# Attention's residual made in the gate stage, and down projections that open with two fetched pages and fetch the rest among their weights

## The chip, the cores and the metric

The kernel is one program on one of the eight cores of a Trainium2 chip. The metric is the time of one execution on the device in microseconds (us); three executions of the kernel before are at hand, and one more was taken by the hardware profiler.

The engines have short names here: PE (TensorE, matrix products), DVE (VectorE), ACT (ScalarE), POOL (GpSimd) and SP (SyncE, which in this kernel issues every DMA, in the order of its program).

## What is computed

Two layers over 1024 tokens of width 1024, in float32. Layer 0 mixes tokens with a gated MLP, layer 1 with a neighbourhood attention; each layer goes on with a convolutional FFN and a gate:

```python
for i in range(DEPTH):
    mix = spatial_gating_mixer(x, ...) if i % 2 == 0 else neighbourhood_attention(x, ...)   # o @ w_o + b_o
    x = layer_norm(DEEPNORM_ALPHA * x + mix, ln1_g[i], ln1_b[i])
    ffn = conv_ffn(x, ...)          # (gelu(a) * g) @ w_down + b_down, hidden width 2816 = 22 pages of 128
    x = layer_norm(DEEPNORM_ALPHA * x + ffn, ln2_g[i], ln2_b[i])
    gate = jax.nn.sigmoid(x @ ple_w_gate[i] + ple_b_gate[i])
    x = x + gate * (p[i] @ ple_w_proj[i])
```

So attention's residual is ALPHA times the output of layer 0's gate, plus the bias b_o.

## The kernel before, in words

**Products.** Each float32 operand is split in two parts, `hi` (a rounded copy, made by ACT, line 90) and `lo` (the remainder, made by DVE, line 91). `mm3` (lines 113 to 118) makes a product from three matmuls: hi by hi, hi by lo, lo by hi. A matmul here has 512 columns. A "page" is 128 of the contracted channels for all 1024 tokens, 512 KB.

**Order.** The program is written with a tile library that puts instructions in order on each engine and inserts the waits; a tile with a tag has a fixed number of buffers (`wr`, raw weights, 2; `wh` and `wl`, split weights, 3 each; `bc` 3), and a new tile waits until the oldest buffer's readers are done. Eight semaphores serve the DMAs in turn, so SP issues one only when the DMA eight before it has landed.

**finish, tm_part1, tm_part2** (lines 425, 169 and 203) are the last step of each mixer and of each FFN: a product with tokens on the partitions, residual, layer norm. `tm_part1` runs over two column halves h, and in each over the pages `ks` but the last three, two pages to a chunk: a chunk's weights are loaded to `wr` and split, the two pages are split into a ring of eight buffers in a big tile, and PE runs 48 matmuls (8 token blocks, 2 pages, 3 each). The four PSUM tiles of a half are then added to `acc` by DVE, eight additions (line 201), and only this frees them for the other half. `acc` is filled beforehand with the residual: a DMA for each of 8 token blocks, and a DVE operation ALPHA * acc + bias (line 421). The first page of the mixers without a reordered store, and of the FFN, is split into two `bc` buffers named `yf` (line 428). `tm_part2` does the last three pages and the layer norm.

**ffn** (line 516) makes the up projection in 22 steps; from step 3 on each is seven products of half size (`seven`, line 454), followed by the convolution, gelu and gate in `evac` (line 574). Pages 0 to 19 of the result go to DRAM (`yd`), 20 and 21 stay in SBUF. The down projection takes its pages in the order 20, 21, 18, 19, 0 to 17; lines 615 to 623 first issue the DMAs that fetch all pages back, then the eight for `acc` (from `xb`, the layer norm's output), then call `finish`.

**ple** (line 628) is the gate. In layer 0 each of its eight channel blocks x is split for the next stage, transposed by PE (`turn`, line 674) and stored to DRAM as `xres`, tokens by channels.

**attention** (line 715) does eight head pairs. Their outputs are gathered by POOL in a tile `tmp` (line 866) and stored as page `oT[hp]`. After the last pair, lines 914 to 922 load `acc` from `xres` in eight DMAs, each a grid block of 8 rows by 16 tokens, make the residual with bias row R_BO, and load the eight `oT` pages to `yo`. `finish` then takes pages 0 to 4 in `tm_part1` and 5 to 7 in `tm_part2`.

Of the kernel before, what the change touches and what calls it, by code (L numbers as in the profile page):

```python
# [9 lines left out]
F32 = mybir.dt.float32  # L10
F32R = mybir.dt.float32r
AF = mybir.ActivationFunctionType
# [4 lines left out]
P = 128  # L17
T = 1024
D = 1024
NT = T // P  # L20
# [5 lines left out]
R = 3  # L26
ALPHA = 4.0 ** 0.25
# [7 lines left out]
C_GATE = C_QKV + 24  # L35
NCOL = C_GATE + 16


(R_BV, R_SG, R_SB, R_BS, R_BOUT, R_BO) = (0, 2, 4, 6, 7, 8)
R_L = 9  # L40


class Trunk:
# [123 lines left out]


    def tm_part1(self, w, y, ks, acc, ring, residual, prep):

        nc = self.nc
        i = ri = 0
        for h in range(2):
            pss = [self.ps() for _ in range(4)]
            for c in range(0, len(ks), 2):
                kk = ks[c : c + 2]
                wh, wl = self.chunk(w[h, kk[0] : kk[-1] + 1].rearrange("k p f -> p k f"), (P, len(kk), 512))
                yy = []
# [235 lines left out]

    def residual(self, acc, row):
        b = []

        def scale(t):
            if not b:
                b.append(self.row(row))  # L420
            self.nc.vector.scalar_tensor_tensor(acc[:, t, :], acc[:, t, :], ALPHA, b[0], op0=ALU.mult, op1=ALU.add)

        return scale

    def finish(self, ringslot, w, y, K, acc, residual, which, X, cols=None, xb=None):

        rg = self.slot(ringslot, F32R)
        first = xb is None and [self.wp.tile([P, T], F32R, tag="bc", name=self.name("yf"), bufs=3) for _ in range(2)]
        ring = lambda i: (rg[:, 2 * (i % 4), :], rg[:, 2 * (i % 4) + 1, :]) if i or not first else first
        ks = list(range(K)) if isinstance(K, int) else K  # L430
# [10 lines left out]

        self.tm_part1(w, y, ks[:-R], acc, ring, residual, prep)
        layer, ln2 = divmod(which, 2)
# [72 lines left out]
    def ffn(self, layer, X, old, new):  # L516
# [8 lines left out]
        B |= {n: (q(TH, i, j), q(TL, i, j)) for n, i, j in (("T1", 0, 0), ("T2", 0, 1), ("T3", 1, 0), ("T4", 1, 1))}  # L525
        HOME = {16: 2, 17: 4, 18: 3, 19: 5}
        cnt = {"wh": 0, "wl": 0}
# [87 lines left out]
        yb = [self.slot(new[0], F32), self.slot(new[1], F32)]  # L615
        ks = [20, 21, 18, 19] + list(range(18))
        for k in (18, 19, *range(18)):
            y[k] = yb[k // 8][:, k % 8, :] if k < 16 else self.single(HOME[k], F32)
            nc.sync.dma_start(y[k], yd[k])
        acc = self.slot(old[0], F32)  # L620
        for t in range(NT):
            nc.sync.dma_start(acc[:, t, :], self.xb[t])
        residual = self.residual(acc, R_L + 5 * layer + 2)
        return self.finish(old[1], a["w_down"][layer], lambda k: y[k], ks, acc, residual, 2 * layer + 1,
                           lambda: (self.slot(new[0], F32R), self.slot(new[1], F32R)))


    def ple(self, layer, X, new):
# [30 lines left out]
        def evac(j, ps, pj, sl=slice(0, T)):  # L659
            s = self.tmp()[:, sl]  # L660
            x = self.single(4 if new else (j + sl.start // 512) % 4, F32)[:, sl]
            nc.gpsimd.tensor_tensor(x, XH[:, j, sl].bitcast(F32), XL[:, j, sl].bitcast(F32), op=ALU.add)
            psf = ps.rearrange("p h f -> p (h f)")[:, sl]
            c = C_GATE + 8 * layer + j
            nc.scalar.activation(s, psf, AF.Sigmoid, bias=self.cols[:, c : c + 1])
            nc.vector.tensor_tensor(s, s, pj[:, sl], op=ALU.mult)
            nc.vector.tensor_tensor(x, x, s, op=ALU.add)
            if not new:
                nc.sync.dma_start(self.out[j][:, sl], x)
                return  # L670
            self.split(NH[:, j, :], NL[:, j, :], x)
            self.pend.append(lambda: turn(j, x))

# [41 lines left out]
    def attention(self, X, free, old):  # L715
        nc, a = self.nc, self.a
        fa, fb = self.slot(free[0], F32), self.slot(free[1], F32R)
        qk = [self.single(i, F32R) for i in range(6)]
        oT = self.dp.tile([8, P, T], F32, name="oT")
        fa = fa.rearrange("p k f -> p (k f)")  # L720
# [129 lines left out]
        def values(hp, t):  # L850
# [8 lines left out]
            if t == 0:  # L859
                st["o"] = self.tmp()  # L860
            o = osum[0:64, t % 2]
            nc.scalar.copy(o, ptf[64:128, 0:512])
            nc.vector.tensor_tensor(o, ptf[0:64, 0:512], o, op=ALU.add)
            for e in range(2):
                c = e * 256
                nc.gpsimd.tensor_tensor(st["o"][64 * e : 64 * e + 64, t * P : t * P + P], o[:, c : c + P], o[:, c + P : c + 256], op=ALU.add)
            if t == 7:
                nc.sync.dma_start(oT[hp], st["o"])
# [114 lines left out]
def prep(i):  # L983
# [3 lines left out]
    o = {}  # L987
# [51 lines left out]
    colv += [np.asarray(i["ple_b_gate"])[l] for l in range(2)]  # L1039
    o["cols"] = c(np.concatenate([v.reshape(-1, P) for v in colv]).T)  # L1040
    rows = [np.asarray(i["sg_b_in"])[0, E:], np.asarray(i["sg_ln_g"])[0], np.asarray(i["sg_ln_b"])[0],
            np.asarray(i["sg_b_s"])[0], np.asarray(i["sg_b_out"])[0], np.asarray(i["na_b_o"])[0]]
    for l in range(2):
# [21 lines left out]
```

## Time and profile before

| what | value |
|---|---|
| median of 3 executions | 2722.09 us (2720.78 to 2722.97) |
| the profiled execution's own time | 2721.23 us |
| its span, first to last instruction | 2719.5 us |
| mean granted TensorE clock | 0.994 of full |
| PE busy | 2671.1 us (98%) |
| DVE busy | 1714.2 us (63%) |
| ACT busy | 1086.1 us (40%) |
| DMA | 238.36 MB, mean 88 GB/s |

Times in the trace are counted from the first instruction. The time of an execution holds 1.7 us more than the span. An engine's row names the tile that it writes, then those that it reads, and in brackets how long the engine stood idle before it and what ended that; PE's clock is given as a share of the full 2.4 GHz. In this program layer 0's FFN ends its up projection at 998 us, layer 0's gate runs from 1282 to 1392 us, attention's last product begins at 1831 us, and layer 1's FFN ends its up projection at 2370 us.

### The profile page before, as it was taken

The page shows a single profiled execution, that of the slowest core. Times are in us where ns is not written, and L with a number is a line of the kernel's source. Part 1 is how long each engine was busy: PE and PEld are TensorE (multiplying, and loading weights), DVE is VectorE, ACT ScalarE, POOL GpSimd, SP SyncE. Part 2 cuts the span into 40 slices and gives each one's busy share as a digit, 9 for nine tenths or more (in the row PEclk, how much of TensorE's full clock was granted, in tenths as well). Part 3 has the DMA queues.
Part 4 walks back from the last instruction along what each step waited for, and adds up shares of the span by engine and source line. Part 5 has one row for each costly group of instructions (what it writes and reads, how often), then busy time and mean ns, then how long its engine had stood idle before and what let it go on. Part 6 is the DMA issues. An engine that isn't in the chain of part 4 may idle for free.

```text
span 2719.5 us, 31562 instructions
## 1 busy us (share of the span) xinstructions
PE 2671.1 (98%) x12536; PEld 2196.1 (81%) x12536; DVE 1714.2 (63%) x2223; ACT 1086.1 (40%) x1475; POOL 350.6 (13%) x372
## 2 busy tenths in 40 slices
PE   9999999999999999999999999997999999999999
PEld 7888888888888878888887777776888888788887
DVE  3247554498787864347437767685887877743373
ACT  3234222344444442224335555572444444522231
POOL 0013320010000000002124333340200000000031
PEclk9999999999999999999999999998999999999999
DMA  5111131222222263121321111154312222451113
GB/s 177 55 55 41 42 132 51 81 86 70 88 76 93 70 223 139 52 61 36 102 87 55 40 47 55 36 175 146 94 68 88 83 80 93 149 203 54 43 55 124
DMA packets 86660, 238.36 MB, mean 88 GB/s; under 512 B 7536, under 2 KB 19696, under 8 KB 86512
## 3 DMA queue, kind: packets, MB, share of 16 engines
q1 hardware_dynamic: 86512, 236.34, 25.6%
q8 instruction: 98, 1.61, 0.3%
q14 instruction: 50, 0.41, 0.0%
HBM read 190.18 MB, written 46.14 MB: 87 GB/s over the span
## 4 chain that ended last, share of the span: by engine, by line
PE 92%; DVE 4%; ACT 1%; DMA 1%; issue 1%; POOL 0%; SPq 0%; DVEq 0%; ACTq 0%
PE ps L116 20%; PE ps L118 20%; PE ps L117 20%; PE bank L117 9%; PE bank L116 9%; PE bank L118 9%; PE ps L845 1%; PE ps L857 1%; PE ps L827 1%; PE ps L235 1%; DMA bc<-in_rows 1%; ACT bigA L831 1%; DVE bigA L835 1%; DVE bigB L91 0%; ACT wh L90 0%
## 5 line engine op out<-in xcount | busy, mean ns | idle before, releaser
L91 DVE TENSOR_TENSOR wl<-wr,wh 128x1024 fp32r<-128x1024 f32 (+2 forms) x227 | 247.2, 1090 | 274.5 <-ACT wh L90 274.0
L90 ACT CAST wh<-wr 128x1024 fp32r<-128x1024 f32 (+2 forms) x227 | 212.1, 935 | 336.9 <-PE ps L117 136.8
L224 POOL TENSOR_SCALAR st<-st 128x1 f32<-128x1 f32 x32 | 34.1, 1065 | 1598.6 <-ACT ps L223 1598.6
L116 PE MATMUL ps<-wh,bigD 128*128 128x512 f32 x592 | 230.3, 389 | 0.0
L118 PE MATMUL ps<-wh,bigD 128*128 128x512 f32 x592 | 230.3, 389 | 0.0
L117 PE MATMUL ps<-wl,bigD 128*128 128x512 f32 x592 | 230.3, 389 | 0.0
L117 PE MATMUL ps<-bigD,wh 128*128 128x512 f32 x544 | 214.6, 394 | 0.0
L116 PE MATMUL ps<-bigA,wh 128*128 128x512 f32 x512 | 200.7, 392 | 0.9 <-DVE tmp L387 0.9
L118 PE MATMUL ps<-bigA,wl 128*128 128x512 f32 x512 | 199.4, 389 | 0.0
L116 PE MATMUL ps<-bigC,wh 128*128 128x512 f32 x480 | 199.2, 415 | 0.0
L118 PE MATMUL ps<-bigC,wl 128*128 128x512 f32 x480 | 190.5, 397 | 0.0
L118 PE MATMUL ps<-wh,bigB 128*128 128x512 f32 x456 | 178.3, 391 | 0.0
L117 PE MATMUL bank<-bigD,wh 128*128 128x512 f32 x456 | 177.4, 389 | 0.0
L116 PE MATMUL ps<-wh,bigA 128*128 128x512 f32 x336 | 133.0, 396 | 19.7 <-DVE bigC L201 14.8
L117 PE MATMUL ps<-bigB,wh 128*128 128x512 f32 x384 | 149.5, 389 | 0.0
L117 PE MATMUL ps<-wl,bigA 128*128 128x512 f32 x336 | 132.7, 395 | 0.0
L116 PEld LDWEIGHTS ps<-wh,bigD 128*128 128x128 f32 x592 | 111.1, 188 | 23.3
L117 PEld LDWEIGHTS ps<-wl,bigD 128*128 128x128 f32 x592 | 111.1, 188 | 23.0
L118 PEld LDWEIGHTS ps<-wh,bigD 128*128 128x128 f32 x592 | 111.1, 188 | 23.0
L116 PE MATMUL bank<-bigA,s 128*128 128x512 f32 x304 | 118.3, 389 | 0.0
L118 PE MATMUL bank<-bigA,s 128*128 128x512 f32 x304 | 118.3, 389 | 0.0
L116 PE MATMUL bank<-bigA,wh 128*128 128x512 f32 x304 | 118.3, 389 | 0.0
(286 smaller groups left out, 6371.2 us busy)
## 6 DMA issues: line engine op xcount, KB each, us to landing
wr<-in_w_up SPq DMA_DIRECT2D x88, 512.0 KB
wr<-in_w_down SPq DMA_DIRECT2D x42, 512.0 KB
yd<-s SPq DMA_DIRECT2D x40, 512.0 KB
wr<-in_w_qkv SPq DMA_DIRECT2D x24, 512.0 KB
bc<-in_rows SPq DMA_DIRECT2D x18, 512.0 KB
wr<-in_w_u SPq DMA_DIRECT2D x16, 512.0 KB
bigA<-yd SPq DMA_DIRECT2D x16, 512.0 KB
wr<-in_w_gate SPq DMA_DIRECT2D x16, 512.0 KB
```

The costliest lines, as they stand in the source:

```text
L90: self.nc.scalar.copy(hi, x)
L91: self.nc.vector.tensor_tensor(lo, x, hi.bitcast(F32), op=ALU.subtract)
L116: mm(out, lh, rh, start=start, stop=False)
L117: mm(out, lh, rl, start=False, stop=False)
L118: mm(out, ll, rh, start=False, stop=stop)
L224: nc.gpsimd.tensor_scalar(st[:, 3:4], st[:, 2:3], 1.0 / D, EPS, op0=ALU.mult, op1=ALU.add)
L235: nc.tensor.transpose(pt[:, kb], a[:, kb], self.ident)
L827: nc.tensor.matmul(ps[:, e, 0:n], qs[es, t * P : t * P + P], kv(ks, es), start=i == 0, stop=i == 2)
L831: nc.scalar.activation(L[:, e, 0:n], L[:, e, 0:n], AF.Exp, bias=sm[:, e : e + 1], scale=-1.0, accum_out=sm[:, 2 + e : 3 + e])
L835: nc.vector.tensor_scalar(L[:, e, 0:n], L[:, e, 0:n], sm[:, 4 + e : 5 + e], None, op0=ALU.mult)
L845: nc.tensor.transpose(ptf[0:m, c : c + P], L[:, e, b * m : b * m + m], self.ident)
L857: nc.tensor.matmul(ptf[:, e * 256 : e * 256 + 256], fv[0:m, blk, e].rearrange("p s d -> p (s d)"), ph[:, 2 * b + e].rearrange("p s q -> p ...
```

## The change

Three parts.

1. **Attention's residual.** In layer 0's gate, ACT turns each channel block x, once it is split, into ALPHA * x + b_o in place, so `xres` holds attention's whole residual. Attention's `acc` is loaded by the same eight DMAs, now issued from `tm_part1`, with no DVE operation after them and no bias row loaded. (b_o moves from the table of rows to the table of columns.)
2. **Attention's last page.** POOL writes the output of the last head pair to `yo` itself, not to `tmp`; it isn't stored to DRAM and fetched back. The other seven pages are fetched earlier in the program's text.
3. **Down projections.** The pages are taken in the order 18, 19, 20, 21, 0 to 17. Pages 18 and 19 are fetched from DRAM through `wr` buffers, and their splits go to two pairs of `wh`/`wl` buffers; the second chunk's weights go to two single tiles instead. The other pages, and the eight blocks of `acc`, are fetched where they are used, among the weights, and no longer ahead of them all.

```diff
@@ tm_part1
-                wh, wl = self.chunk(w[h, kk[0] : kk[-1] + 1].rearrange("k p f -> p k f"), (P, len(kk), 512))
+                src = w[h, kk[0] : kk[-1] + 1].rearrange("k p f -> p k f")
+                if early and h == 0 and c == 2:
+                    wh, wl = self.single(2, F32R), self.single(4, F32R)
+                    self.split(wh, wl, self.raw(src, (P, 2, 512)))
+                else:
+                    wh, wl = self.chunk(src, (P, len(kk), 512))
@@ residual
+            if src is not None:
+                self.nc.sync.dma_start(acc[:, t, :], src[t])
             self.nc.vector.scalar_tensor_tensor(acc[:, t, :], acc[:, t, :], ALPHA, b[0], op0=ALU.mult, op1=ALU.add)
@@ finish
-        first = xb is None and [self.wp.tile([P, T], F32R, tag="bc", name=self.name("yf"), bufs=3) for _ in range(2)]
-        ring = lambda i: (rg[:, 2 * (i % 4), :], rg[:, 2 * (i % 4) + 1, :]) if i or not first else first
+        part = lambda tag: self.wp.tile([P, T], F32R, tag=tag, name=self.name(tag), bufs=3)
+        early = which % 2 == 1
+        first = []
+        if early:
+            first = [(part("wh"), part("wl")) for _ in range(2)]
+        elif xb is None:
+            first = [(part("bc"), part("bc"))]
+        ring = lambda i: (rg[:, 2 * (i % 4), :], rg[:, 2 * (i % 4) + 1, :]) if i >= len(first) else first[i]
@@ ffn
-        ks = [20, 21, 18, 19] + list(range(18))
-        for k in (18, 19, *range(18)):
-            y[k] = yb[k // 8][:, k % 8, :] if k < 16 else self.single(HOME[k], F32)
-            nc.sync.dma_start(y[k], yd[k])
+        ks = [18, 19, 20, 21] + list(range(18))
+        def yk(k):
+            seen[k] = seen.get(k, 0) + 1
+            if k in (18, 19) and seen[k] == 1:
+                return self.raw(yd[k])
+            if k not in y:
+                y[k] = yb[k // 8][:, k % 8, :] if k < 16 else self.single(HOME[k], F32)
+                nc.sync.dma_start(y[k], yd[k])
+            return y[k]
         acc = self.slot(old[0], F32)
-        for t in range(NT):
-            nc.sync.dma_start(acc[:, t, :], self.xb[t])
-        residual = self.residual(acc, R_L + 5 * layer + 2)
+        residual = self.residual(acc, R_L + 5 * layer + 2, self.xb)
@@ ple
             self.split(NH[:, j, :], NL[:, j, :], x)
+            nc.scalar.activation(x, x, AF.Identity, bias=self.cols[:, C_BO + j : C_BO + j + 1], scale=ALPHA)
@@ attention
-                st["o"] = self.tmp()
+                if hp == 7:
+                    yo = st["yo"] = self.slot(old[1], F32)
+                    for k in range(7):
+                        nc.sync.dma_start(yo[:, k, :], oT[k])
+                st["o"] = self.tmp() if hp < 7 else st["yo"][:, 7, :]
...
-            if t == 7:
+            if t == 7 and hp < 7:
                 nc.sync.dma_start(oT[hp], st["o"])
...
-        for t in range(NT):
-            src = grid[t // 4, t % 4]
-            nc.sync.dma_start(acc[:, t, :], src)
-        residual = self.residual(acc, R_BO)
-        yo = self.slot(old[1], F32)
-        for k in range(8):
-            nc.sync.dma_start(yo[:, k, :], oT[k])
+        residual = lambda t: nc.sync.dma_start(acc[:, t, :], grid[t // 4, t % 4])
+        yo = st["yo"]
```

The change shifts line numbers: line 91 before is 92 after, 201 is 207, 421 is 429, 489 is 504, 567 and 568 are 581 and 582, 580 is 594, 619 is 640, 918 is 944.

**SP, where attention ends.** `bigC` is `acc`, `tmp` the last head pair's output, `bigD` is `yo`, `bc` a row, `wr` a buffer for weights. Before:

```order
L101 DMA wr_13269<-in_w_o 128x2x512
L918 DMA bigC_13076<-xres 128x1x1024
L770 DMA pj<-pj_13052 128x1024
L918 DMA bigC_13076<-xres 128x1x1024 x3
L868 DMA oT<-tmp_12792 128x1024
L918 DMA bigC_13076<-xres 128x1x1024 x4
L922 DMA bigD_13085<-oT 128x1024
L81 DMA bc_13167<-in_rows 128x1024
L101 DMA wr_13327<-in_w_o 128x2x512
L101 DMA wr_13385<-in_w_o 128x512
```

After:

```order
L102 DMA wr_13270<-in_w_o 128x2x512
L944 DMA bigC_13096<-xres 128x1x1024
L793 DMA pj<-pj_13073 128x1024
L944 DMA bigC_13096<-xres 128x1x1024 x7
L102 DMA wr_13328<-in_w_o 128x2x512
L82 DMA bc_13450<-in_rows 128x1024
L82 DMA bc_13452<-in_rows 128x1024
L102 DMA wr_13386<-in_w_o 128x512
```

The store of the last page, its fetch and the first row are gone; the eight blocks of `acc` follow one another, and the weights of the second half's second chunk (`wr_13328`, before `wr_13327`) stand right behind them.

**DVE, at the turn from the first column half to the second in attention's last product.** `wl` is the lo part of weights, `ps` the first half's PSUM tiles. Before:

```order
L91 TENSOR_TENSOR wl_13272<-wr_13269,wh_13271 128x1024
L421 SCALAR_TENSOR_TENSOR bigC_13076<-bigC_13076,bc_13167 128x1024 x8
L201 TENSOR_TENSOR bigC_13076<-ps_13095,bigC_13076 128x512 x2
L201 TENSOR_TENSOR bigC_13076<-ps_13096,bigC_13076 128x512 x2
L201 TENSOR_TENSOR bigC_13076<-ps_13097,bigC_13076 128x512 x2
L201 TENSOR_TENSOR bigC_13076<-ps_13098,bigC_13076 128x512 x2
L91 TENSOR_TENSOR bigA_13094<-bigD_13085,bigA_13094 128x1024
L91 TENSOR_TENSOR wl_13330<-wr_13327,wh_13329 128x1024
```

After:

```order
L92 TENSOR_TENSOR wl_13273<-wr_13270,wh_13272 128x1024
L92 TENSOR_TENSOR bigA_13097<-bigD_12806,bigA_13097 128x1024
L92 TENSOR_TENSOR wl_13331<-wr_13328,wh_13330 128x1024
L207 TENSOR_TENSOR bigC_13096<-ps_13098,bigC_13096 128x512 x2
L207 TENSOR_TENSOR bigC_13096<-ps_13099,bigC_13096 128x512 x2
L207 TENSOR_TENSOR bigC_13096<-ps_13100,bigC_13096 128x512 x2
L207 TENSOR_TENSOR bigC_13096<-ps_13101,bigC_13096 128x512 x2
```

The eight residual operations are gone, and the split of the second chunk's weights has moved from behind the eight additions to ahead of them.

**DVE, where layer 0's down projection begins.** `up` are the last step's results, `s_745` is page 20 and `s_765` page 21. Before:

```order
L489 TENSOR_TENSOR up_6631<-bank_6632,up_6631 128x1024
L567 SCALAR_TENSOR_TENSOR s_765_6727<-up_6630,cols,s_765_6727 128x1023
L91 TENSOR_TENSOR wl_6904<-wr_6901,wh_6903 128x1024
L568 SCALAR_TENSOR_TENSOR s_765_6727<-up_6630,cols,s_765_6727 128x1023
L567 SCALAR_TENSOR_TENSOR tmp_6733<-up_6631,cols,tmp_6733 128x1023
L570 TENSOR_TENSOR s_765_6727<-s_765_6727,cve_1069 128x2
L91 TENSOR_TENSOR yf_6776<-s_745_6592,yf_6775 128x1024
```

After (`wr_6761` is page 19, `wr_6815` the second chunk's weights, `bigC` is `acc`):

```order
L504 TENSOR_TENSOR up_6631<-bank_6632,up_6631 128x1024
L582 SCALAR_TENSOR_TENSOR s_765_6727<-up_6630,cols,s_765_6727 128x1023
L92 TENSOR_TENSOR wl_6746<-wr_6761,wh_6745 128x1024
L584 TENSOR_TENSOR s_765_6727<-s_765_6727,cve_1069 128x2
L581 SCALAR_TENSOR_TENSOR tmp_6733<-up_6631,cols,tmp_6733 128x1023
L92 TENSOR_TENSOR s_785_6814<-wr_6815,s_784_6813 128x1024
L582 SCALAR_TENSOR_TENSOR tmp_6733<-up_6631,cols,tmp_6733 128x1023
L429 SCALAR_TENSOR_TENSOR bigC_6741<-bigC_6741,bc_6823 128x1024
L584 TENSOR_TENSOR tmp_6733<-tmp_6733,cve_1069 128x2
L429 SCALAR_TENSOR_TENSOR bigC_6741<-bigC_6741,bc_6823 128x1024
L594 TENSOR_TENSOR s_765_6727<-s_765_6727,tmp_6733 128x1024
```

The split of page 20, which the first matmuls read before, is no longer behind the last step's convolution; page 18's split (not shown) stands four rows further up, and page 19's takes its place.

## Rows read from the trace of the kernel before

**Rows 1.** The page: busy time by engine, and PE's clock in 40 slices.
```profile
PE 2671.1 (98%) x12536; PEld 2196.1 (81%) x12536; DVE 1714.2 (63%) x2223; ACT 1086.1 (40%) x1475; POOL 350.6 (13%) x372
PEclk9999999999999999999999999998999999999999
```

**Rows 2.** The waits of PE: released by; us in total, times, longest us.
```profile
PE ps L116 <- DVE bigC L201: 15.5, 2, 14.8
PE ps L118 <- DVE yf L91: 10.4, 2, 5.2
```

**Rows 3.** The timeline of PE, layer 0's down projection: start us, us, instruction [idle before].
```profile
997.56 0.39 PE L118 MATMUL bank<-bigA,wl 128*128 128x512 f32 x1
997.78 0.39 PE L116 MATMUL ps<-wh,yf 128*128 128x512 f32 x1
...
998.92 0.39 PE L117 MATMUL ps<-wl,yf 128*128 128x512 f32 x1
...
1005.60 0.79 PE L118 MATMUL ps<-wh,yf 128*128 128x512 f32 x1 [5.19 <-DVE yf L91]
...
1011.70 0.40 PE L116 MATMUL ps<-wh,bigD 128*128 128x512 f32 x1
```

**Rows 4.** The timeline of DVE in the same stretch.
```profile
998.40 1.22 DVE L489 TENSOR_TENSOR up<-bank,up 128x1024 f32<-128x1024 f32 x1
999.54 1.27 DVE L567 SCALAR_TENSOR_TENSOR s<-up,cols,s 128x1023 f32<-128x1023 f32 x1
1000.73 1.21 DVE L91 TENSOR_TENSOR wl<-wr,wh 128x1024 fp32r<-128x1024 f32 x1
...
1004.32 1.22 DVE L91 TENSOR_TENSOR yf<-s,yf 128x1024 fp32r<-128x1024 f32 x1
```

**Rows 5.** The timeline of PE in attention's last product, at the turn of the halves.
```profile
1858.18 0.39 PE L118 MATMUL ps<-wh,bigA 128*128 128x512 f32 x1
1873.33 0.77 PE L116 MATMUL ps<-wh,bigA 128*128 128x512 f32 x1 [14.76 <-DVE bigC L201]
...
1877.68 0.39 PE L116 MATMUL ps<-wh,bigA 128*128 128x512 f32 x1
```

**Rows 6.** The chain that ended last, in the same place: start us, us, what.
```profile
1837.23 6.97 DMA oT<-tmp
...
1844.58 18.20 DMA bc<-in_rows
```

**Rows 7.** The timelines of SP, DVE and ACT there.
```profile
1827.17 0.76 SPq L918 DMA_DIRECT2D bigC<-xres  x1
...
1862.81 9.17 DVE L421 SCALAR_TENSOR_TENSOR bigC<-bigC,bc 128x1024 f32<-128x1024 f32 x8 [17.30 <-DMA bc<-in_rows]
1871.90 4.87 DVE L201 TENSOR_TENSOR bigC<-ps,bigC 128x512 f32<-128x512 f32 x8
...
1864.13 1.04 ACT L90 CAST wh<-wr 128x1024 fp32r<-128x1024 f32 x1 [10.82 <-DMA wr<-in_w_o]
```

**Rows 8.** Stretches: us; busy of PE, PEld, DVE, ACT, POOL (instructions); PEclk; DMA share, GB/s.
```profile
997.78:1011.70 13.92, 8.37 (x26) 6.06 (x24) 12.61 (x13) 5.73 (x6) 0.00 (x0) 0.75 0.99 388
1858.41:1877.68 19.27, 4.51 (x11) 3.51 (x11) 14.87 (x17) 3.46 (x4) 0.00 (x0) 0.56 0.21 80
...
1000.00:1036.00 36.00, 30.81 (x126) 24.93 (x125) 19.16 (x19) 8.12 (x8) 0.00 (x0) 0.91 1.01 398
...
1840.00:1844.00 4.00, 4.00 (x19) 3.30 (x19) 0.86 (x1) 1.94 (x2) 0.00 (x0) 1.00 0.52 211
1844.00:1859.00 15.00, 14.56 (x65) 11.72 (x63) 1.50 (x2) 1.12 (x2) 0.00 (x0) 1.00 0.98 222
```

**Rows 9.** The timeline of PE: the turn of the halves in layer 0's down projection.
```profile
1213.91 0.47 PE L116 MATMUL ps<-s,bigD 128*128 128x512 f32 x1 [0.76 <-DVE bigC L201]
```

**Rows 10.** ACT alone in layer 0's gate: us, ACT busy (instructions), PEclk, DMA share, GB/s.
```profile
1282.00:1392.00 110.00, 33.00 (x35) 1.00 0.34 102
```

More of the change, by code (lines that the diff above doesn't have):

```diff
@@ L35 @@
 C_GATE = C_QKV + 24
-NCOL = C_GATE + 16
-(R_BV, R_SG, R_SB, R_BS, R_BOUT, R_BO) = (0, 2, 4, 6, 7, 8)
-R_L = 9
+C_BO = C_GATE + 16
+NCOL = C_BO + 8
+(R_BV, R_SG, R_SB, R_BS, R_BOUT) = (0, 2, 4, 6, 7)
+R_L = 8
 class Trunk:
@@ L166, in ws_blocks, with tm_part1 @@
             evac(j, ps)
-    def tm_part1(self, w, y, ks, acc, ring, residual, prep):
+    def tm_part1(self, w, y, ks, acc, ring, residual, prep, early):
         nc = self.nc
@@ L413, in gmlp, with residual @@
         return self.finish("B", a["w_out"], lambda k: y[k], NE, acc, residual, 0, lambda: (self.slot("C", F32R), self.slot("D", F32R)))
-    def residual(self, acc, row):
+    def residual(self, acc, row, src=None):
         b = []
@@ L440, in prep @@
                 self.split(*w2[q], r)
-        self.tm_part1(w, y, ks[:-R], acc, ring, residual, prep)
+        self.tm_part1(w, y, ks[:-R], acc, ring, residual, prep, early)
         layer, ln2 = divmod(which, 2)
@@ L525, in ffn @@
         B |= {n: (q(TH, i, j), q(TL, i, j)) for n, i, j in (("T1", 0, 0), ("T2", 0, 1), ("T3", 1, 0), ("T4", 1, 1))}
-        HOME = {16: 2, 17: 4, 18: 3, 19: 5}
         cnt = {"wh": 0, "wl": 0}
@@ L615, in ffn @@
         yb = [self.slot(new[0], F32), self.slot(new[1], F32)]
-        ks = [20, 21, 18, 19] + list(range(18))
-        for k in (18, 19, *range(18)):
-            y[k] = yb[k // 8][:, k % 8, :] if k < 16 else self.single(HOME[k], F32)
-            nc.sync.dma_start(y[k], yd[k])
+        ks = [18, 19, 20, 21] + list(range(18))
+        HOME = {16: 2, 17: 4, 18: 3, 19: 5}
+        seen = {}
+        def yk(k):
[6 more added lines that the diff above has]
+            return y[k]
         acc = self.slot(old[0], F32)
-        for t in range(NT):
-            nc.sync.dma_start(acc[:, t, :], self.xb[t])
-        residual = self.residual(acc, R_L + 5 * layer + 2)
-        return self.finish(old[1], a["w_down"][layer], lambda k: y[k], ks, acc, residual, 2 * layer + 1,
+        residual = self.residual(acc, R_L + 5 * layer + 2, self.xb)
+        return self.finish(old[1], a["w_down"][layer], yk, ks, acc, residual, 2 * layer + 1,
                            lambda: (self.slot(new[0], F32R), self.slot(new[1], F32R)))
@@ L718, in attention @@
         qk = [self.single(i, F32R) for i in range(6)]
-        oT = self.dp.tile([8, P, T], F32, name="oT")
+        oT = self.dp.tile([7, P, T], F32, name="oT")
         fa = fa.rearrange("p k f -> p (k f)")
@@ L1039, in prep @@
     colv += [np.asarray(i["ple_b_gate"])[l] for l in range(2)]
+    colv.append(np.asarray(i["na_b_o"])[0])
     o["cols"] = c(np.concatenate([v.reshape(-1, P) for v in colv]).T)
     rows = [np.asarray(i["sg_b_in"])[0, E:], np.asarray(i["sg_ln_g"])[0], np.asarray(i["sg_ln_b"])[0],
-            np.asarray(i["sg_b_s"])[0], np.asarray(i["sg_b_out"])[0], np.asarray(i["na_b_o"])[0]]
+            np.asarray(i["sg_b_s"])[0], np.asarray(i["sg_b_out"])[0]]
     for l in range(2):
```

## The prediction

> **What bounds the kernel.** I read the page first: PE is busy 98% of the span and its clock stands at full but for one slice of 40 [rows 1]. A matmul of 512 columns costs 0.227 us when nothing is late (six steps from 997.56 to 998.92) [rows 3], and the change keeps all 12536 of them. So it can only move what PE waits. The waits of PE come next: two groups stand out, one of 14.8 us and one of 5.2 us that occurs twice, once in each layer [rows 2]. The timelines place them: at the start of each down projection [rows 3], and at the turn of the column halves in attention's last product [rows 5]. Both are places that the change edits. Each wait costs more than its idle time, because PE resumes at half its clock: the stretches around them show 0.75 and 0.56 of full, that is a time at 1.2 GHz instead of 2.4 [rows 8].
>
> **What the two places are worth.** In the down projection, page 20's 24 matmuls take from 997.78 to 1011.70, 13.92 us; at 0.227 each they need 5.44. The excess is 8.48 us [rows 3], of which 5.19 is the long idle time. The other layer has the same wait [rows 2]: 16.96 for both. In attention the first half's last matmul is through at 1858.41, and from there to 1877.68, 19.27 us, ten matmuls start (2.27 us): excess 17.00 [rows 5, 8]. Together 34.0 us, the most that the change can give back.
>
> **Down projections, step by step.** Before, PE waits for the lo part of page 20, which DVE makes only at 1004.32, behind the last step's convolution [rows 4]. Now the first matmuls read page 18, finished some three up-projection steps earlier, and its split stands ahead of that convolution. What is late next? Page 19: its lo part follows operations of lines 489 and 568 (now 504 and 582); DVE's operations there start at 998.40 and each takes a step of 1.14 to 1.19 us. Its own split starts at 1000.73 and ends about 1001.9 [rows 4]; PE wants it after 24 matmuls, at 997.78 + 5.44 = 1003.2. It is 1.3 us early. Then page 21, at 997.78 + 48 * 0.227 = 1008.7: its convolution now shares DVE with the split of the second chunk's weights and two residual operations. Counting the steps of the order from there (six of 1.14 to 1.19 us, two small ones), its last operation (line 594) ends at 1009.1, ACT's copy at 1010.2, and the lo part, three DVE places later, at 1012.5. PE's program has seven matmuls ahead of the first that reads the hi part and 17 ahead of the first that reads the lo part, so it wants them at 1010.25 and 1012.5. That is neither early nor late; I take 0.3 us a layer, between 0 and 1.
>
> The fetches that now stand among the weights: a chunk lasts PE 10.9 us and needs at most two pages, two blocks of `acc` and one load of weights, 2.6 MB, which take 6.6 us at the 398 GB/s that this place shows before [rows 8]. They are hidden by that margin; without it PE would wait 1.5 us a chunk at the 211 GB/s of the slowest stretch. Pages 18 and 19 are fetched twice a layer, four DMAs of 0.5 MB in the whole kernel, of which the lost store and fetch of attention's last page pay half.
>
> Sum here: 2 * (8.48 - 0.3) = 16.4 us.
>
> **Attention, step by step.** Before, the last page's store (6.97 us) holds up SP, then the bias row needs 18.20 us behind the blocks of `acc` [rows 6], then eight residual operations take 9.17 us, and only then come the eight additions that free PSUM [rows 7]. The change takes all of this away: store, fetch, row and the eight operations. In return ACT gets eight operations in the gate, about 1.05 us each like its copies [rows 7], 8.4 us in a stretch of 110 in which ACT is busy for 33 [rows 10]; the transposes that read their results come a block later, so I price this at nothing, and at 8.4 if that cover failed.
>
> What is late next is the second chunk's weights: their split now stands in DVE ahead of the additions, and their load behind eight blocks of `acc` and one other store, ten transfers of 0.524 MB. The first block's DMA goes out at 1827.17 [rows 7]; no row shows this sequence. From below: at the 211 GB/s of a stretch in which the blocks run nearly alone [rows 8], 5.24 MB last 24.8 us, so the weights land about 1853. From the whole of the sequence before, thirteen transfers ended by ACT's copy at 1864.13, 36.96 us [rows 7]: ten last 28.4 (1855.6), and twelve, if the two layer norm rows get in between, 34.1 (1861.3). Behind the landing stand copy 1.15, split 1.25 and two additions 1.4 us [rows 4, 7], so PE could go on at 1857, 1859.4 or 1865.1. It stops at 1858.6 [rows 5], and the least gap at such a turn is 0.76 [rows 9]. So the wait left is 0.8 to 6.5 us. I take 2.5, between the second and third, since blocks and other loads together ran at 0.98 of the DMA engines' time for only 222 GB/s [rows 8], and here too they run together.
>
> The blocks alone held 0.52 of the DMA engines' time at 211 GB/s, where other loads reach 398 at 1.01 [rows 8]: half the engines. The Trainium skill (DMA: Bandwidth & Descriptors, "Why a DMA increments its semaphore by 16 and not by 1") says that a transfer is dealt over the largest number of engines up to 16 that divides the slowest dimension of both sides; a block's source has 8 rows there. By that rule the trace agrees, and issuing the blocks sooner makes them no faster: the sum by it is that of the first rival.
>
> Sum here: 17.0 - 2.5 = 14.5 us.
>
> **Forecast.** 16.4 + 14.5 = 30.9 us, from the profiled execution's 2721.23 to 2690.3. The median of the three runs is 0.86 above that execution, so 2691.2 us.
>
> **The rivals.**
>
> *The wait in attention turns into one for weights.* For it: the half-engine rate and the new order of DVE. Against: six fewer things stand ahead than before. At the far bound PE idles 6.5 us, and like the 5.19 us idle of the down projection, whose excess was 3.3 more, it resumes at half clock: 9.6 instead of 2.5, so 2698.3 us. Chance 0.25, for waits of over 4 us.
>
> *The down projections keep their waits.* Page 19's copy takes a `wh` buffer that the last up-projection product still reads, and its split is behind DVE's convolution; if DVE there were 3 us later than the rows say, PE would stop again between pages 18 and 19 or 20 and 21, and pay the clock too. With all of the 16.4 lost: 2707.6. Chance 0.11.
>
> *Slower: fetches among weights make a serial loop.* SP issues in order, and a load of weights waits for a `wr` buffer, that is for a split which stands in DVE behind residual operations that wait for blocks of `acc` behind earlier weights. If this left one buffer in effect, a chunk would cost the load, a copy of 1.04, a split of 1.21 and up to five other DVE operations of 1.17 us [rows 4, 7], 8.1 us and the load, against PE's 10.9. A load of 0.5 MB would then have to last 3.7 us, as 142 GB/s would make it, for PE to lose 0.9 us in each of the 40 chunks (ten in each half, two halves, two layers), which takes the gain of 30.9 and 5.4 more; at a loss of 1.0 us it ends at 2691.2 + 40 = 2731. Against it: two buffers, only the first four chunks of a first half have residual work, and the place shows 398 GB/s [rows 8]. Chance 0.03.
>
> *It does nothing.* Every new wait takes what the old one held, because the order of DVE and not the pages or the row set it: 2722. The rows of DVE's idle time there speak against that [rows 7]. Chance 0.04.
>
> **Numbers.** The forecast's case, with a wait of under 4 us in attention, has 0.57. Its own range is 2687.6 (least gap, no wait for page 21, runs spread 1.3 below the median as before) to 2695.5. The range that I give goes on through the first rival and a part of the second: 2687 to 2702. A difference of 0.2%, 5.4 us, is about what a measurement of this kernel can tell from none. Faster by more than that: the forecast's case and the first two rivals, 0.93; within it 0.04; slower 0.03.
>
> **What would show it.** In the changed profile the wait behind `yf` is gone in both layers, page 18's matmuls follow the last up-projection product without a gap, and no wait over 1 us stands in the first two chunks. At the turn of attention's halves a wait of some 2.5 us stands behind line 207, and before that DVE waits on the split of `wr` weights, not on a row. The clock stays full in both places. I am wrong if a wait over 4 us remains at any of the three, if waits recur at each chunk of a down projection, or if the gate's stretch grows by over 1 us.

## The result and the profile after

The changed kernel took 2691.28 us (median; 2690.34 to 2692.40), beside 2722.53 us for the kernel before: a ratio of 0.9889, 95% interval 0.9876 to 0.9903, or 31.25 us less. The forecast was 2691.2 us. A later series gave 2695.23 us (2692.72 to 2703.76) beside 2720.26 us, ratio 0.9908 (0.9893 to 0.9923): the gain is there each time, but its size moved by 6 us. The experiments show why.

The changed kernel's busy time by engine and its PE clock answer to [rows 1]:

```profile
PE 2665.3 (99%) x12536; PEld 2194.1 (82%) x12536; DVE 1704.2 (63%) x2215; ACT 1095.3 (41%) x1483; POOL 350.4 (13%) x372
...
PEclk9999999999999999999999999999999999999999
```

Its waits of PE (columns as in [rows 2]):

```profile
PE ps L117 <- ACT wh L91: 5.0, 1, 5.0
...
PE ps L117 <- DVE bigC L207: 2.4, 2, 1.6
...
PE ps L702 <- ACT s L694: 0.5, 1, 0.5
```

Both large groups of [rows 2] are gone. The wait of 5.0 is the program's start, which the kernel before has too. Of the 14.8 us at attention's turn 1.6 are left, and a wait of 0.5 us in the gate is new.

**Down projection.** The timelines of PE, ACT and DVE in layer 0 answer to [rows 3, 4]:

```profile
997.61 0.39 PE L119 MATMUL bank<-bigA,wl 128*128 128x512 f32 x1
997.84 0.39 PE L117 MATMUL ps<-wh,wh 128*128 128x512 f32 x1
...
1008.72 0.39 PE L117 MATMUL ps<-s,bigD 128*128 128x512 f32 x1
...
1009.18 1.05 ACT L91 CAST bigD<-s 128x1024 fp32r<-128x1024 f32 x1 [1.51 <-DVE s L594]
...
1007.92 1.22 DVE L594 TENSOR_TENSOR s<-s,tmp 128x1024 f32<-128x1024 f32 x1
...
1011.33 1.22 DVE L92 TENSOR_TENSOR bigD<-s,bigD 128x1024 fp32r<-128x1024 f32 x1
```

Pages 18 and 19 take from 997.84 to 1008.72, 10.88 us for 48 matmuls: 0.227 each, nothing is late. Page 21's last DVE operation ends at 1009.1, its copy at 1010.2, its lo part at 1012.55.

**Attention's turn.** The timelines of SP, ACT, DVE and PE answer to [rows 5, 7]:

```profile
1821.63 7.71 SPq L944 DMA_DIRECT2D bigC<-xres  x7
1829.44 0.40 SPq L102 DMA_DIRECT2D wr<-in_w_o  x1
...
1850.70 1.05 ACT L91 CAST wh<-wr 128x1024 fp32r<-128x1024 f32 x1 [3.22 <-DMA wr<-in_w_o]
...
1851.79 1.22 DVE L92 TENSOR_TENSOR wl<-wr,wh 128x1024 fp32r<-128x1024 f32 x1 [3.04 <-ACT wh L91]
1852.93 4.87 DVE L207 TENSOR_TENSOR bigC<-ps,bigC 128x512 f32<-128x512 f32 x8
...
1854.36 0.47 PE L117 MATMUL ps<-wh,bigA 128*128 128x512 f32 x1 [1.61 <-DVE bigC L207]
```

The weights are issued at 1829.44 and copied at 1850.70, 21 us later; split and additions follow at once, and PE waits behind them.

**Where the time went.** Both programs run the same 12536 matmuls, so the start of the n-th in one trace can be set against that in the other. The lead grows by 8.3 us at layer 0's down projection, shrinks by 0.7 in the gate, by 0.3 in attention's preparation and by 1.5 just after 1823, grows by 15.1 at attention's turn and by 8.3 at layer 1's down projection: 29.2, and the spans differ by 29.4 (2719.5 and 2690.1).

The 1.5 us is clock. The same stretch of the changed kernel in this execution and in a second one, from the later series (columns as in [rows 8]):

```profile
1823.37:1826.78 3.41, 3.41 (x12) 2.83 (x12) 3.40 (x5) 3.41 (x5) 2.81 (x2) 0.50 0.52 171
```

```profile
1823.37:1826.78 3.41, 3.41 (x19) 2.82 (x18) 3.40 (x5) 3.41 (x5) 2.82 (x2) 1.00 0.52 160
```

In both executions PE had just idled 1.83 us, until 1822.96. The first then ran 3.41 us at 1.2 GHz, the second at 2.4. The kernel before has the same idle time and goes on at full clock. So this term belongs to the execution, not to the change.

### The profile page after: what moved, and what is told of

It reads as the page before. It is cut to its first block, busy times and chain, and to the rows that moved or that the text cites. A ratio compares the mean times of both kernels' runs of the same rounds, so it can differ in the third digit from the quotient of the medians.

```text
span 2690.1 us, 31562 instructions
## 1 busy us (share of the span) xinstructions
PE 2665.3 (99%) x12536; PEld 2194.1 (82%) x12536; DVE 1704.2 (63%) x2215; ACT 1095.3 (41%) x1483; POOL 350.4 (13%) x372
## 3 DMA queue, kind: packets, MB, share of 16 engines
q8 instruction: 98, 1.61, 0.2%
## 4 chain that ended last, share of the span: by engine, by line
PE 93%; DVE 3%; ACT 1%; DMA 1%; issue 1%; SPq 0%; DVEq 0%; ACTq 0%
PE ps L117 20%; PE ps L118 20%; PE ps L119 20%; PE bank L118 9%; PE bank L117 9%; PE bank L119 9%; PE ps L880 1%; PE ps L868 1%; PE ps L850 1%; PE ps L241 1%; DMA wr<-in_w_o 1%; ACT bigA L854 1%; DVE bigA L858 1%; ACT wh L91 0%; DVE bigB L92 0%
## 5 line engine op out<-in xcount | busy, mean ns | idle before, releaser
L230 POOL TENSOR_SCALAR st<-st 128x1 f32<-128x1 f32 x32 | 34.1, 1065 | 1568.4 <-ACT ps L229 1568.4
L118 PE MATMUL ps<-wl,bigD 128*128 128x512 f32 x544 | 211.8, 389 | 0.0
L119 PE MATMUL ps<-wh,bigD 128*128 128x512 f32 x544 | 211.8, 389 | 0.0
L117 PE MATMUL ps<-wh,bigD 128*128 128x512 f32 x544 | 211.8, 389 | 0.0
L119 PEld LDWEIGHTS ps<-wh,bigD 128*128 128x128 f32 x544 | 102.2, 188 | 21.3
L118 PEld LDWEIGHTS ps<-wl,bigD 128*128 128x128 f32 x544 | 102.2, 188 | 21.2
L117 PEld LDWEIGHTS ps<-wh,bigD 128*128 128x128 f32 x544 | 102.2, 188 | 20.9
L854 ACT ACTIVATE bigA<-bigA,st 128x288 f32<-128x288 f32 (+1 forms) x128 | 72.7, 569 | 113.6 <-DVE st L852 113.5
L119 PE MATMUL bank<-bigA,wl 128*128 128x512 f32 x304 | 118.4, 389 | 0.0
L119 PE MATMUL bank<-bigA,s 128*128 128x512 f32 x304 | 118.4, 389 | 0.0
```

Source lines behind the costliest of these rows:

```text
L117: mm(out, lh, rh, start=start, stop=False)
L118: mm(out, lh, rl, start=False, stop=False)
L119: mm(out, ll, rh, start=False, stop=stop)
L230: nc.gpsimd.tensor_scalar(st[:, 3:4], st[:, 2:3], 1.0 / D, EPS, op0=ALU.mult, op1=ALU.add)
L854: nc.scalar.activation(L[:, e, 0:n], L[:, e, 0:n], AF.Exp, bias=sm[:, e : e + 1], scale=-1.0, accum_out=sm[:, 2 + e : 3 + e])
```

## The experiments

**Each part alone.** First attention alone: down projections as before.

```diff
-        early = which % 2 == 1
+        early = False
...
-        ks = [18, 19, 20, 21] + list(range(18))
+        ks = [20, 21, 18, 19] + list(range(18))
...
+        for k in (18, 19, *range(18)):
+            y[k] = yb[k // 8][:, k % 8, :] if k < 16 else self.single(HOME[k], F32)
+            nc.sync.dma_start(y[k], yd[k])
...
```

> Edit: the changed kernel with the down projections of the kernel before (old page order, all fetches ahead of the weights). Theory (the two gains are separate and add): only attention's excess goes, 17.0 less the 1.6 us wait and its restart that the changed profile still has, less 0.7 us that the gate's longer ACT chain costs: 13 to 15 us faster than before, 2707.5 to 2709.5 us; the two 5.19 us waits behind yf are still there. Rival (the gains depend on each other, by the order in which the scheduler puts the whole program): the attention wait is over 4 us here, 2712 us or more.

Then the down projections alone: gate and attention as before.

```diff
-            nc.scalar.activation(x, x, AF.Identity, bias=self.cols[:, C_BO + j : C_BO + j + 1], scale=ALPHA)
...
-                st["o"] = self.tmp() if hp < 7 else st["yo"][:, 7, :]
+                st["o"] = self.tmp()
...
-            if t == 7 and hp < 7:
+            if t == 7:
...
```

> Edit: the changed kernel with gate and attention of the kernel before. Theory: both down projections lose their whole excess of 8.48 us, 2722.5 - 16.9 = 2705.6 us (2704.5 to 2706.5), attention's 14.8 us wait stays, and no PE wait over 0.5 us in the gate. Rival (part of the gain came from the shorter queues around it): 2708 us or more.

Attention alone: 2709.16 us, ratio 0.9950 (0.9933 to 0.9966), as expected. Down projections alone: 2704.33 us, 0.9929 (0.9914 to 0.9944), 0.2 us below the expected range. PE's waits, attention alone and then down projections alone:

```profile
PE ps L119 <- DVE bc L92: 10.4, 2, 5.2
...
PE ps L117 <- DVE bigC L207: 3.8, 2, 3.1
```

```profile
PE ps L117 <- DVE bigC L207: 15.5, 2, 14.8
```

The spans are shorter than before by 12.4 us (2707.1) and 17.1 us (2702.4), 29.5 together, where the whole change has 29.4: the gains add. The gate's 0.7 us stands in the first trace and not in the second. At the turn itself attention alone leads by 13.7 us, and the whole change by 15.1 less the 1.5 that the clock had taken just before. Attention's wait is 3.1 us here and 1.6 in the whole change, though the attention code is the same: with attention alone the clock stayed full behind the same 1.83 us (columns as in [rows 8]), and PE came to the turn that much sooner.

```profile
1831.40:1834.81 3.41, 3.41 (x18) 2.84 (x18) 3.40 (x5) 3.41 (x5) 2.81 (x2) 1.00 0.51 183
```

**Attention's two parts.** First the residual made by DVE with a bias row again, last page kept in SBUF:

```diff
-            nc.scalar.activation(x, x, AF.Identity, bias=self.cols[:, C_BO + j : C_BO + j + 1], scale=ALPHA)
...
-        residual = lambda t: nc.sync.dma_start(acc[:, t, :], grid[t // 4, t % 4])
+        residual = self.residual(acc, R_BO, [grid[t // 4, t % 4] for t in range(NT)])
```

> Edit: the changed kernel, but attention's residual is made by eight DVE operations with a bias row again (part 1 undone); the last page stays in SBUF (part 2 kept). Theory A (the row and the eight operations cost by themselves): the row adds one transfer to the queue, the last block lands about 1851.5, then one residual operation, three splits and the first two additions, 6 to 7 us, stand in DVE before PE can go on: idle of 5 to 7 us at the turn instead of 1.6, with the half-clock restart 2696 to 2699 us. Theory B (only the blocked queue behind the store mattered, the operations hide behind the blocks' landings): idle under 3 us, 2691 to 2693 us.

Then the last page stored and fetched again, residual from the gate:

```diff
-                st["o"] = self.tmp() if hp < 7 else st["yo"][:, 7, :]
+                st["o"] = self.tmp()
...
-            if t == 7 and hp < 7:
+            if t == 7:
...
+        yo = self.slot(old[1], F32)
+        for k in range(8):
+            nc.sync.dma_start(yo[:, k, :], oT[k])
```

> Edit: the changed kernel, but the last page is stored and fetched again (part 2 undone); the residual still comes finished from the gate (part 1 kept). Theory A: SP stands at the store for some 7 us with four blocks behind it, the blocks end about 1854 and the weights of the second half's second chunk about 1856, then copy, split and two additions: idle of 5 to 8 us at the turn, 2696 to 2701 us. Theory B (what cost was the row and the eight operations): idle under 3 us, 2691 to 2693 us. If this run and the one with the row back both end near A, the two parts each take about half of what attention lost, and neither alone gives it all.

With the row: 2697.24 us (2695.66 to 2699.20). With the store: 2699.20 us (2697.50 to 2699.73). DVE and PE with the row, then SP, ACT and PE with the store:

```profile
1848.84 1.23 DVE L429 SCALAR_TENSOR_TENSOR bigC<-bigC,bc 128x1024 f32<-128x1024 f32 x1 [1.65 <-DMA bigC<-xres]
1849.98 1.22 DVE L92 TENSOR_TENSOR wl<-wr,wh 128x1024 fp32r<-128x1024 f32 x1
1851.11 2.35 DVE L92 TENSOR_TENSOR bigA<-bigD,bigA 128x1024 fp32r<-128x1024 f32 x2
1853.38 1.22 DVE L92 TENSOR_TENSOR wl<-wr,wh 128x1024 fp32r<-128x1024 f32 x1
1854.52 4.87 DVE L207 TENSOR_TENSOR bigC<-ps,bigC 128x512 f32<-128x512 f32 x8
...
1855.95 0.76 PE L117 MATMUL ps<-wh,bigA 128*128 128x512 f32 x1 [4.89 <-DVE bigC L207]
```

```profile
1822.22 2.35 SPq L939 DMA_DIRECT2D bigC<-xres  x3
1830.45 0.32 SPq L891 DMA_DIRECT2D oT<-tmp  x1
1830.81 1.22 SPq L939 DMA_DIRECT2D bigC<-xres  x2
1837.84 0.32 SPq L942 DMA_DIRECT2D bigD<-oT  x1
...
1839.52 1.14 SPq L102 DMA_DIRECT2D wr<-in_w_o  x2
...
1855.16 1.04 ACT L91 CAST wh<-wr 128x1024 fp32r<-128x1024 f32 x1 [7.06 <-DMA wr<-in_w_o]
...
1858.81 0.76 PE L117 MATMUL ps<-wh,bigA 128*128 128x512 f32 x1 [5.45 <-DVE bigC L207]
```

Both times lie in the range of theory A, and the rows show its two paths. With the row, the residual operations hide behind the blocks' landings, but the last one and the splits that queue behind it do not. With the store, SP stands from 1824.6 to 1830.45 until the page is complete and from 1832.0 to 1837.84 until the store has landed, and the weights go out at 1839.52, 10 us later than in the changed kernel. Waits of 4.89 and 5.45 us come back, and the medians lie 6.0 and 7.9 us above 2691.28 (2.0 and 4.0 above the 2695.23 of the later series). Of the 15.1 us that the change gains at the turn, 9.8 and 8.5 are left: the first part undone costs 5.4 us, the second 6.7, and both undone [rows 6, 7] cost all of it. What each part costs is less sure than its path: the changed kernel itself waited 4.13 us in the later series, as is seen below.

**Order of the pages, place of the fetches.**

```diff
-        ks = [18, 19, 20, 21] + list(range(18))
+        ks = [20, 21, 18, 19] + list(range(18))
```

> Edit: the changed kernel with the down projections' old page order, 20, 21, 18, 19 (fetches still stand among the weights). Theory A (the order of the pages is what removed the wait, since pages 20 and 21 come last out of the up projection): DVE's order now has ten operations of 1.15 us ahead of the lo part of page 21, which ends near 1012 us where PE wants it at 1003 to 1007; 5 to 8 us of idle and the half-clock restart come back in each layer: 2707 to 2713 us. Theory B (the early fetches took DMA time and DVE time at the start, and spreading them is what helped): under 2696 us.

```diff
...
+        for k in range(16):
+            y[k] = yb[k // 8][:, k % 8, :]
+            nc.sync.dma_start(y[k], yd[k])
         acc = self.slot(old[0], F32)
-        residual = self.residual(acc, R_L + 5 * layer + 2, self.xb)
+        for t in range(NT):
+            nc.sync.dma_start(acc[:, t, :], self.xb[t])
+        residual = self.residual(acc, R_L + 5 * layer + 2)
```

> Edit: the changed kernel, but pages 0 to 15 and the eight blocks of acc are fetched ahead of the down projection's loop, as before; the new page order stays. Theory A (fetches among the weights are needed once the first wait is gone): the weights of the third chunk stand behind 24 transfers of 0.5 MB, 31.6 us at 398 GB/s from 998 us, and land about 1031 to 1033; copy and split end near 1035, but PE wants them at 997.8 + 2 * 10.9 = 1019.6: an idle of 13 to 16 us and a restart at half clock in each layer, 2716 to 2730 us, all of the gain of the down projections gone or more. Theory B (the new order alone does it, the place of the fetches is neutral): 2690 to 2693 us.

The old order: 2715.10 us (2714.10 to 2722.64), ratio 0.9970 (0.9957 to 0.9982). The fetches ahead: 2725.14 us (2723.82 to 2731.58), ratio 1.0012 (1.0002 to 1.0022), so a little slower than the kernel before. ACT and PE with the old order, then SP, ACT and PE with the fetches ahead, and last SP in the kernel before, all in layer 0:

```profile
1010.59 1.04 ACT L91 CAST wh<-s 128x1024 fp32r<-128x1024 f32 x1 [3.79 <-DVE s L594]
...
1011.68 0.80 PE L117 MATMUL ps<-wh,wh 128*128 128x512 f32 x1 [8.01 <-ACT wh L91]
```

```profile
974.75 0.33 SPq L102 DMA_DIRECT2D wr<-yd  x1
...
987.48 0.32 SPq L102 DMA_DIRECT2D wr<-yd  x1
994.75 0.38 SPq L102 DMA_DIRECT2D wr<-in_w_down  x1
...
998.26 4.36 SPq L645 DMA_DIRECT2D bigA<-yd  x8
...
1022.09 1.67 SPq L102 DMA_DIRECT2D wr<-in_w_down  x2
...
1032.40 1.04 ACT L91 CAST wh<-wr 128x1024 fp32r<-128x1024 f32 x1 [11.22 <-DMA wr<-in_w_down]
...
1033.50 1.22 PE L117 MATMUL ps<-wh,bigD 128*128 128x512 f32 x2 [13.44 <-ACT wh L91]
```

```profile
974.65 0.38 SPq L101 DMA_DIRECT2D wr<-in_w_down  x1
...
987.39 0.38 SPq L101 DMA_DIRECT2D wr<-in_w_down  x1
...
994.66 0.38 SPq L101 DMA_DIRECT2D wr<-in_w_down  x1
...
998.12 4.88 SPq L619 DMA_DIRECT2D bigA<-yd  x8
```

Theory A in both, with the old order some 2 us beyond its upper end: the wait was 8.0 us, the most that was expected, and this kernel's profiled execution, at 2722.64 us the slowest of its six, also had 9.8 us at attention's turn. The third chunk's weights behind the fetches are copied at 1032.4, where a landing from 1031 to 1033 was expected. They stand there because pages 18 and 19 now take `wr` buffers: before, four loads of weights went out ahead of the fetches (the first at 971.52), and now two (the other one at 971.60). So the two halves of part 3 need each other. Set against the kernel before, a down projection with the old order loses 1.4 us in layer 0 and 1.6 in layer 1, one with the fetches ahead loses 8.0 and 7.9, and with both halves it gains 8.3.

**What is left at attention's turn.** First the second chunk's weights loaded ahead of most blocks:

```diff
...
                     last = c + 2 >= len(ks)
+                    if last and ahead:
+                        for c1 in (0, 2):
+                            pre[1, c1] = self.raw(w[1, ks[c1] : ks[c1 + 1] + 1].rearrange("k p f -> p k f"), (P, 2, 512))
...
```

> Edit: the changed kernel; in attention's last product the second half's second chunk of weights is loaded behind the second block of acc, not behind the eighth. Theory A (the 1.6 us wait that is left at the turn is the wait for these weights, whose split stands ahead of the additions): the split is done long before, the wait falls to the 0.75 us that the turns of the FFN have, 0.8 us less, 2690 to 2691 us; the additions then wait for nothing but PE. Theory B (the additions wait for the blocks of acc themselves): the blocks land one transfer later, and the wait stays or grows to 2 to 3 us.

Then the residual written in grid order, to the tile `s` in place of `x`, so that a block is 128 rows in a row:

```diff
-            nc.scalar.activation(x, x, AF.Identity, bias=self.cols[:, C_BO + j : C_BO + j + 1], scale=ALPHA)
-            self.pend.append(lambda: turn(j, x))
+            xv = x.rearrange("p (rt r ct c) -> p rt ct r c", rt=2, r=8, ct=4)
+            sv = s.rearrange("p (rt ct r c) -> p rt ct r c", rt=2, r=8, ct=4)
+            for rt in range(2):
+                nc.scalar.activation(sv[:, rt], xv[:, rt], AF.Identity, bias=self.cols[:, C_BO + j : C_BO + j + 1], scale=ALPHA)
+            self.pend.append(lambda: turn(j, s))
...
-        residual = lambda t: nc.sync.dma_start(acc[:, t, :], grid[t // 4, t % 4])
+        residual = lambda t: nc.sync.dma_start(acc[:, t, :], self.xres[t])
```

> Edit: the changed kernel; the gate writes the finished residual in grid order (two ACT operations of 512 columns in place of one of 1024), so that a block of acc is 128 rows in a row in DRAM instead of 8 groups of 16. Theory A (the blocks are slow because their first dimension of 8 deals them over half the DMA engines): a block's share of the engines doubles, eight blocks and the weights take about 1.3 us each and have landed by 1836, the wait at the turn falls to 0.75 us: 2690 to 2691.5 us, with up to 1 us more for the gate's extra ACT operations. Theory B (the blocks are slow for another reason, their issue on SP or the reading of DRAM): landings as in the changed kernel, the last near 1849, wait 1.6 us.

Weights first: 2688.38 us (2687.00 to 2688.77), ratio 0.9871 (0.9856 to 0.9886). Grid order: 2687.42 us (2686.08 to 2689.99), ratio 0.9870 (0.9855 to 0.9884). Both are below their expected ranges. ACT and DVE with the weights first:

```profile
1846.11 1.04 ACT L91 CAST wh<-wr 128x1024 fp32r<-128x1024 f32 x1
...
1848.52 4.87 DVE L212 TENSOR_TENSOR bigC<-ps,bigC 128x512 f32<-128x512 f32 x8
```

The copy waits for nothing, the additions begin at 1848.52, while PE is still in the first half (its matmuls go on through the turn, 0.68 us for each three), and PE has no wait there at all. The lead at the turn is 17.0 us, the whole excess. Theory A is right in kind, and its 0.75 us floor is wrong.

The blocks' stretch with the grid order, and a stretch of the old blocks with the weights first (columns as in [rows 8]):

```profile
1818.90:1831.50 12.60, 11.25 (x52) 9.42 (x53) 8.27 (x8) 6.23 (x8) 5.90 (x5) 1.00 1.00 375
```

```profile
1842.00:1849.00 7.00, 7.00 (x32) 5.82 (x31) 2.76 (x3) 2.95 (x3) 0.00 (x0) 1.00 0.52 209
```

The same blocks move at 375 GB/s with the DMA engines fully busy; the old ones moved at 209 with a share of 0.52. For each unit of busy share the rate is about the same (375 and 402), so the old blocks kept fewer engines busy; their packets were not slower. That is theory A. The Trainium skill (DMA: Bandwidth & Descriptors, "Why a DMA increments its semaphore by 16 and not by 1") has the number of engines as the largest up to 16 that divides the slowest dimension of both sides, 8 for the old blocks and 16 for 128 rows; by that rule the trace agrees.

The last three ran side by side. The changed kernel again, and the grid order again:

> The changed kernel as it is, to stand beside the other two on the same chip. Theory: 2690 to 2693 us; the wait at attention's turn is not a fixed figure, since the same attention code showed 1.6, 3.1, 3.3 and 9.8 us of it in four kernels, with blocks landing at 163 to 222 GB/s: here again between 0.8 and 5 us. Rival (it is fixed by the program, and the other kernels differed by their own edits): 1.6 us again, within 0.2.

> The kernel with the residual in grid order once more, beside the changed kernel on the same chip. Theory (the blocks over all DMA engines take the wait at attention's turn away, and with two half operations of ACT that write another tile the gate's 0.5 us wait is gone too): 2 to 5 us faster than the changed kernel, 2686 to 2689 us, no wait over 0.5 us at the turn nor in the gate. Rival (the first run of it was a lucky one): within 1 us of the changed kernel.

And the gate's residual made by DVE behind the transposes, together with the weights first:

```diff
-            nc.scalar.activation(x, x, AF.Identity, bias=self.cols[:, C_BO + j : C_BO + j + 1], scale=ALPHA)
...
-            nc.scalar.copy(o, ptf)
+            bo = br[0][:, j * P : j * P + P].rearrange("p (o f) -> p o f", o=1).broadcast_to([P, NT, P])
+            nc.vector.scalar_tensor_tensor(o.rearrange("p (t f) -> p t f", t=NT), ptf.rearrange("p (t f) -> p t f", t=NT), ALPHA, bo, op0=ALU.mult, op1=ALU.add)
...
```

> Edit: the kernel with the second chunk's weights ahead of the blocks, and besides it the gate's residual made behind the transposes, by one DVE operation with a bias row that takes the place of ACT's copy out of PSUM, so that ACT has eight operations less. Theory A (the gate's wait of 0.5 us and its 0.7 us are ACT's longer chain ahead of the transposes): the wait is gone, 0.7 us less than with the weights ahead alone (2688.4), 2687 to 2688.5 us. Theory B (DVE becomes what the gate waits for, 1.2 us more in each block): a new PE wait behind DVE in the gate, 2689 us or more.

The changed kernel took 2695.23 us, 2 us above the expected range. The grid order took 2687.16 us (2686.20 to 2687.54; ratio to before 0.9874, 0.9861 to 0.9887), and the two ranges don't meet: side by side the version in grid order beats the changed kernel by 8.1 us, more than the 2 to 5 expected, and the 2691.28 of the first series by 4.1. The traces put 6.8 us of it at the turn, where the grid order's lead is 17.0 again, and 0.6 in the gate. The changed kernel's turn in this series:

```profile
1851.68 1.04 ACT L91 CAST wh<-wr 128x1024 fp32r<-128x1024 f32 x1 [5.74 <-DMA wr<-in_w_o]
...
1855.32 0.77 PE L117 MATMUL ps<-wh,bigA 128*128 128x512 f32 x1 [4.13 <-DVE bigC L207]
```

4.13 us in place of 1.61, so the wait is not fixed by the program. The weights came 1.0 us later, and PE came 1.6 us sooner, since it had not lost that to the clock at 1823: what the clock takes there, the wait had hidden. Five traces have this attention code. In each, PE goes on 3.65 us after the weights' copy begins, and it stops 31.4 us after the first block's issue, or 33.0 where the clock had fallen. That adds up to the wait in all five:

| kernel | first block's issue to the weights' copy, us | clock behind the 1.83 us | wait at the turn, us |
|---|---|---|---|
| changed kernel | 30.9 | half | 1.61 |
| attention alone | 30.8 | full | 3.08 |
| fetches ahead | 31.0 | full | 3.28 |
| changed kernel, later series | 31.9 | full | 4.13 |
| old page order | 37.5 | full | 9.79 |

The gate with DVE: 2689.42 us (2686.21 to 2690.38), inside theory B's range, but this decides nothing beside 2688.38 from another series. Its trace does: set against the run with the weights first it leads by 0.7 us after the gate, no wait of PE in the gate reaches 0.4 us, and it loses 1.2 us in attention's preparation to a wait for ACT's copy of `pj` (1.14 us). Such a wait, of 0.9 to 1.8 us, stands in some of the traces here and not in others (the weights-first run has none). That is theory A for the gate; the time alone was too coarse.

Why the gate waited is in the timelines of ACT and PE, of the changed kernel and then of the grid order:

```profile
1285.45 1.05 ACT L91 CAST bigC<-s 128x1024 fp32r<-128x1024 f32 x1 [4.08 <-DVE s L688]
1287.79 1.15 ACT L694 ACTIVATE s<-s,cols 128x1024 f32<-128x1024 f32 x1 [1.29 <-DVE bigD L92]
...
1289.00 1.09 PE L702 MATMUL ps<-ident,s 128*128 128x128 f32 x8 [0.50 <-ACT s L694]
```

```profile
1284.35 1.05 ACT L91 CAST bigC<-s 128x1024 fp32r<-128x1024 f32 x1 [2.62 <-DVE s L688]
1285.31 1.33 ACT L697 ACTIVATE tmp<-s,cols 128x512 f32<-128x512 f32 x2
```

The new operation writes x (here `s`) in place, so it must wait until DVE's split has read x. With another tile as its output, and as two halves, it follows the copy at once, and PE has no wait.

## Why the prediction was right

- **Down projections.** Forecast 16.4 us, found 8.3 + 8.3 = 16.6. Page 21's chain was forecast to end at 1009.1, 1010.2 and 1012.5 and ended at 1009.1, 1010.2 and 1012.55; of the 0.3 us a layer that I took for it, 0.2 occurred (the lead falls from 8.44 to 8.24 us between 1009.5 and 1015). The cover for the fetches held (358 GB/s in the first 13.6 us, PE's clock full), and the run with the fetches ahead shows its price when it is gone: 13 us of idle a layer.
- **Attention.** Forecast 14.5, found 15.1 at the turn, or 13.6 without the 1.5 that the clock had taken just before. The wait that took the old one's place was the one named, for the second chunk's weights: forecast 2.5 us, found 1.61, and 3.08 where the clock had stayed full. Ten transfers took 30.9 us from the first block's issue (1819.80) to ACT's copy (1850.70), between my second bound (28.4) and third (34.1). The mechanism was shown by loading those weights first: the wait goes, with the blocks as slow as before (209 GB/s).
- **A term that was wrong: the least gap of 0.76.** I took the FFN's turn [rows 9] as a floor. Where the weights are early, the additions free PSUM while PE is still in the first half, and the gap is nothing. This put the own range's low end 0.8 us too high.
- **A term that was missed: the gate.** I priced ACT's eight operations at nothing, since the transposes come a block later. They cost 0.7 us, at one block, because of the wait for DVE's split.
- **The sum.** 30.9 forecast; the two profiled executions differ by 29.4, which to 0.2 us is 16.6 + 15.1 less 0.7 (gate), 0.3 (preparation) and 1.5 (clock). The median moved by 31.25. That the forecast met it to 0.1 us is chance: the later series moved by 25.0.
- **The rivals.** The first one, a wait of over 4 us at the turn, is real in some executions: 4.13 us and a restart at half clock in the later series. The lost down projection did not come about; the old page order and the fetches ahead show that it was one edit away. The serial loop did not come about either, and no run shows it.
- **Slips in the sums.** The first bound's landing is 1852.0 by its own figures (1827.17 + 24.8), not 1853; the first rival's idle of 6.5 us and 3.3 more make 9.8 and 2698.5, not 9.6 and 2698.3; and by SP's two orders three fewer transfers stand ahead of the weights, not six. None of them moves the forecast.

Two things stay open: why the clock falls behind the same idle time in some executions and not in others, and why the ten transfers took 37.5 us (163 GB/s) in the trace of the old page order, where the other four took 30.8 to 31.9 (195 to 200 GB/s).

## What to carry to other kernels

When a buffer gets a new user, look at what it used to carry early: here pages 18 and 19 took the places of two loads of weights, and the new page order lost 8 us a layer until the fetches ahead of those weights were spread among them. Give a small, urgent load (weights) a place ahead of large ones that share its issuing queue, and lay out a reordered block in DRAM so that its DMA is one run of many rows. An operation in place inherits the wait for every earlier reader of the tile; a free tile as output took the wait away here, and with it 0.6 to 0.7 us.

## What the runs showed of the hardware

- Blocks of 8 by 16 rows moved at 209 GB/s with a DMA share of 0.52, the same bytes as 128 rows in a row at 375 GB/s with 1.00. A weight load behind the slow blocks took 21 us from issue to copy.
- The same idle time of PE, 1.83 us, was followed by 3.41 us at 1.2 GHz in one execution and by none in another of the same kernel. It stands in all thirteen traces here, and in the 3.41 us that begin 0.41 us behind it the mean granted clock was 0.50 to 0.53 in four of them, 0.68 in one and full in eight.
- An idle of 4.13 us at the turn, in the later series, cost more than itself: from the end of the first half on, 13 matmuls took 9.31 us instead of 2.95, with a mean granted clock of 0.63. An idle of 3.08 us at the same place, with attention alone, was followed by full clock.
